# Second block: the normalised activations are split, and the conv taps read PSUM

## The chip, the cores and the metric

The kernel runs on one core of a Trainium2 chip. Each engine (TensorE or PE, VectorE or DVE, ScalarE or ACT, GpSimd or POOL, and SyncE or SP, which here mostly issues DMAs) works through its own queue in order and waits for the others at semaphores. The time is device microseconds (us) of one execution; the median of three runs stands for a kernel.

## What is computed

The reference runs two blocks and returns a normalised result. `first_block` has two layers of pooling, sparse attention and memory attention, all behind an RMS norm. The change lies in `second_block`:

```python
h_res = concat([meta_tokens (16), x (256)])             # T = 272 tokens, D = 1024
h = rmsnorm(h_res, norm1_w)                             # per token
q, k, v, z, b_raw, a_raw, sc_b, sc_c, sc_x, gate_a, gate_b = split(h @ w_in)
q, k, v = silu(depthwise_conv_centred([q, k, v], conv_w))    # 5 taps along tokens
q, k = l2norm(q), l2norm(k)
# gated delta rule, forward and backward, in chunks of 64:
#   decay, L = strict(beta * k k^T * decay), T = (I + L)^-1, state update per chunk
y_a = (norm(o_fwd + o_bwd) * silu(z)) @ w_branch_dn
y_b = (sc_b * depthwise_conv_centred(sc_c * sc_x, sc_conv_w)) @ w_branch_sc   # 3 taps
merged = sigmoid(gate_a) * y_a + sigmoid(gate_b) * y_b
h_res = h_res + merged @ w_out ;  then an MLP and a last norm
```

Everything is float32. Each product is made of three matmuls of a type that keeps fewer bits: both operands are split into a high part H and a low part L (value minus H), and H·H, H·L and L·H are summed in PSUM.

## The kernel before

Activations lie with channels on the 128 partitions (KT = 8 groups of 128) and tokens along the row. All weights come over SP's queue in pieces of 128x4x256 (`load`, L94, five buffers `raw`). `weights` splits each piece: `wH` is a copy on ScalarE (L107), `wL` the difference on VectorE, and for every third piece in block two on GpSimd (L110); four buffers each. `unit` and `unit2` make the product of one weight block with the split activations, 24 matmuls per half of 128 outputs (L123), into PSUM tiles `mm`, of which there are four. `units` (L151) does the same for two blocks together, k by k but the last two, so that work can begin before the last channels of x are there.

In `_block2` the operand is the split of x·fn and meta·n1, where `fn` is the product of two norm weights: **it is not divided by each token's root mean square yet**. The row `St` (L635) has that scale for all 272 tokens. It comes from squares summed over channels by a matmul with ones (`st`, L631), a root on ScalarE and a reciprocal on VectorE, while the first matmuls (`pk`, two blocks of k) run. Each result is then multiplied by St as it is taken from PSUM:

```python
V.tensor_tensor(r[:, a:], pss[i][:, :T - a], St[:, a:], op=OP.mult)      # rc, L672
ACT.activation(ac[:, lo:], r[:, lo:], AF.Copy, scale=w[:, 2:3])           # L680
ACT.activation(a4[:, lo:T - 2], r[:, lo + 2:], AF.Copy, scale=w[:, 4:5])  # L681
G.tensor_tensor(ac[:, lo:T - 2], ac[:, lo:T - 2], a4[:, lo:T - 2], op=OP.add)  # L682
```

and three more taps follow on VectorE (L685, result `ac` for q and k, `vf` for v). The twelve units of q, k and v have 24 halves, so 72 such taps. The same scaling is done for `ba` (L754), z (`zs`, L1167), the gates (L1161) and, in the short convolution, for `cS` on VectorE (L1188) and again on GpSimd (L1189, since sc_c and sc_x are multiplied) and for `cv` on GpSimd (L1201).

`delta()` is a generator that is advanced between units. It makes l2 norms (squares `l2s` L703, matmul `l2p` L705, logs and exponentials `rn`), the products `kq` (L713, every third on GpSimd), decays `E` (L897, L899) and the masked matrices (L909, L910, L923). The triangular inverse of the 32x32 corners follows: 31 pairs `tm` and `Tb` (L828, L830) on VectorE, and a small one for the meta tokens, `mt`, on GpSimd. The result, copied to `Lb` (L943), goes through memory and back over SP's queue (`sT` L946, `Tn` L998, `TBX` L1000, `TT` L1003), so that the larger inverse can begin on TensorE (`x`, L1016). Ahead of `x` stand the meta tokens' states: `mkv` (L976 on VectorE, L980 on ScalarE), `mvn` (L979) and `ms` (L984) on TensorE.

A scheduler sets the order of each engine's instructions when the program is built. It simulates the engines with a model of costs, so the order of the code and the order on an engine differ. The pool `ap2` of the second block takes the memory of the first block's pool, and its first writers are five DMAs that ScalarE issues (`cw` and others, L583); the pool of the split operand `xH`, `xL` exists from the start.

## Time and profile before

| | us |
|---|---|
| median of 3 runs | 1180.85 |
| the runs | 1182.15, 1174.7, 1180.85 |
| the profiled execution | 1179.4 |
| its span, first to last instruction | 1177.4 |
| TensorE busy | 1114.1 (95%) |
| VectorE busy | 869.0 (74%) |
| ScalarE busy | 586.7 (50%) |
| GpSimd busy | 383.5 (33%) |
| mean granted clock of TensorE | 0.979 |

Busy times add up instructions, and matmuls overlap, so a busy TensorE is not one at its peak. Block one ends near 571 us; block two's mixers run from there to about 940, with the MLP behind. The granted clock is a share of full speed (2.4 GHz; the lower level is 1.2).

### The profile page before, as it was taken

Reading aid. Unit: us, or ns where it says so; the run is one execution under the profiler, and the core shown is the slowest. Engines: PE = TensorE matmul, PEld = TensorE weight load, DVE = VectorE, ACT = ScalarE, POOL = GpSimd, SP = SyncE. Lnnn points to the kernel's source line nnn. Section 1 sums busy time; section 2 is a strip of 40 time slices with the busy share of each in tenths; the row PEclk is TensorE's granted clock in tenths of the full one; section 3 lists DMA queues with packets and bytes.
Section 4 is the critical chain, followed back from the end, with each engine's and each line's share of the span. In section 5 each row is a group of like instructions: output and inputs, shape, how many; then the busy total and the mean of one; then the engine's idle time right before and its main releaser. Section 6 shows DMA issues by size and latency. Waiting matters only on the chain.

```text
span 1177.4 us, 23260 instructions
## 1 busy us (share of the span) xinstructions
PE 1114.1 (95%) x9536; PEld 1086.1 (92%) x9536; DVE 869.0 (74%) x1220; ACT 586.7 (50%) x883; POOL 383.5 (33%) x304
## 2 busy tenths in 40 slices
...
GB/s 262 268 211 170 156 173 123 180 192 182 196 192 182 179 133 136 147 177 180 186 169 144 181 82 144 134 175 105 148 126 94 134 187 180 200 172 199 180 193 40
DMA packets 68514, 194.63 MB, mean 165 GB/s; under 512 B 19504, under 2 KB 21816, under 8 KB 67896
## 3 DMA queue, kind: packets, MB, share of 16 engines
...
q14 instruction: 32, 0.26, 0.1%
...
## 4 chain that ended last, share of the span: by engine, by line
PE 70%; DVE 17%; DMA 4%; issue 3%; ACT 2%; POOL 2%; SPq 1%; DVEq 0%; ACTq 0%; POOLq 0%
PE mm L123 49%; PE mml L151 8%; PE mmd L1302 5%; DVE wL L110 4%; DVE ac L685 2%; DVE Tb L830 1%; PE hp L372 1%; ACT wH L107 1%; DMA sT<-Lb 1%; DMA rows<-scr 1%; DVE tm L828 1%; DVE vf L685 1%; DVE kq L713 1%; PE mo L495 1%; PE vn L1088 1%
## 5 line engine op out<-in xcount | busy, mean ns | idle before, releaser
L110 DVE TENSOR_TENSOR wL<-raw,wH 128x1024 fp32r<-128x1024 f32 (+2 forms) x292 | 395.9, 1362 | 156.4 <-ACT wH L107 139.4
L107 ACT ACTIVATE wH<-raw 128x1024 fp32r<-128x1024 f32 (+3 forms) x347 | 347.0, 1034 | 302.4 <-PE mm L123 150.2
L123 PE MATMUL mm<-xH,wL 128*128 128x256 f32 (+3 forms) x1720 | 247.7, 284 | 11.2 <-DVE wL L110 11.2
L123 PE MATMUL mm<-xH,wH 128*128 128x256 f32 (+3 forms) x1720 | 249.0, 286 | 5.6 <-ACT ac L680 1.8
L123 PE MATMUL mm<-xL,wH 128*128 128x256 f32 (+3 forms) x1720 | 248.6, 285 | 0.0
L123 PEld LDWEIGHTS mm<-xH,wL 128*128 128x128 f32 (+1 forms) x1720 | 221.9, 190 | 13.5 <-DVE wL L110 12.3
L123 PEld LDWEIGHTS mm<-xH,wH 128*128 128x128 f32 (+1 forms) x1720 | 222.7, 190 | 9.5 <-ACT ac L680 2.0
L123 PEld LDWEIGHTS mm<-xL,wH 128*128 128x128 f32 (+1 forms) x1720 | 223.2, 191 | 2.8 <-issue 2.2
L110 POOL TENSOR_TENSOR wL<-raw,wH 128x1024 fp32r<-128x1024 f32 (+2 forms) x55 | 133.9, 2434 | 217.5 <-ACT wH L107 149.3
L397 POOL TENSOR_TENSOR bp<-bias,sc 128x1024 f32<-128x1024 f32 (+1 forms) x4 | 14.7, 3667 | 246.3 <-DVE sc L395 219.9
L123 PE MATMUL mm<-yH,wH 128*128 128x256 f32 x256 | 42.5, 286 | 4.9 <-ACT yH L1207 4.9
L123 PE MATMUL mm<-yL,wH 128*128 128x256 f32 x256 | 43.0, 286 | 4.3 <-DVE yL L1208 4.3
L123 PE MATMUL mm<-yH,wL 128*128 128x256 f32 x256 | 42.1, 285 | 0.0
L191 POOL TENSOR_TENSOR acc<-x 128x256 f32<-128x256 f32 x2 | 1.4, 722 | 123.6 <-DVE x L562 120.4
L123 PEld LDWEIGHTS mm<-yH,wH 128*128 128x128 f32 x256 | 35.6, 193 | 5.2 <-ACT yH L1207 5.1
L123 PEld LDWEIGHTS mm<-yL,wH 128*128 128x128 f32 x256 | 35.7, 193 | 5.1 <-DVE yL L1208 4.8
L123 PEld LDWEIGHTS mm<-yH,wL 128*128 128x128 f32 x256 | 35.5, 193 | 0.3 <-issue 0.3
L193 POOL TENSOR_TENSOR sq<-x 128x256 f32<-128x256 f32 x33 | 33.6, 1027 | 6.2 <-DVE x L562 5.5
L685 DVE SCALAR_TENSOR_TENSOR ac<-rc,cw,ac 128x271 f32<-128x271 f32 (+3 forms) x48 | 34.4, 753 | 0.0
L191 POOL TENSOR_TENSOR a<-x 128x256 f32<-128x256 f32 x3 | 2.8, 941 | 80.4 <-DVE x L562 74.8
L1302 PE MATMUL mmd<-aH,wH 128*128 128x256 f32 x176 | 28.6, 281 | 0.0
L1302 PE MATMUL mmd<-aH,wL 128*128 128x256 f32 x176 | 28.6, 281 | 0.0
...
## 6 DMA issues: line engine op xcount, KB each, us to landing
...
```

Source lines behind the costliest of these rows:

```text
L107: nc.scalar.activation(H, raw, AF.Copy)
L110: e.tensor_tensor(L, raw, H.bitcast(F32), op=OP.subtract)
L123: self.last_mm = nc.tensor.matmul(ps, lt(a, kt), rt(b, kt), start=i == 0, stop=i == n - 1).ins
L151: self.last_mm = self.nc.tensor.matmul(ps[:, :N], w[a](k)[:, h * 128:h * 128 + 128], xs[b][:, k, :], start=k == 0 and (a, b) == (0, 0), st ...
L193: nc.gpsimd.tensor_tensor(tmp, x, x, op=OP.mult)
L372: nc.tensor.matmul(pp[p][:, j, :n], a[r, 2 * i + j, :], b(r, 2 * i + j), start=True, stop=True)
L397: nc.gpsimd.tensor_tensor(bp[:, :, :n], bias[:, :, off:], pen[:, None, :n].to_broadcast([128, 8, n]), op=OP.add)
L495: nc.tensor.matmul(ps[:, h, :], mv[:, mb, h * 128:h * 128 + 128], PT[:, mb, h, :], start=mb == 0, stop=mb == 1)
L685: V.scalar_tensor_tensor(ac[:, t0:t1], r[:, t0 + j - 2:t1 + j - 2], w[:, j:j + 1], ac[:, t0:t1], op0=OP.mult, op1=OP.add)
L713: (V if (i * 8 + h) % 3 else G).tensor_tensor(t, t, sl(h, i), op=OP.mult)
L828: eng.tensor_tensor(t, Lb[:, j + 1:, j:j + 1].to_broadcast([P, m, w]), Tb[:, j:j + 1, 0:w].to_broadcast([P, m, w]), op=OP.mult)
L1302: nc.tensor.matmul(pss[h][:, :S], w[a](k)[:, h * 128:h * 128 + 128], (aH, aL)[b][:, k0 + k, :], start=k0 + k == 0 and (a, b) == (0, 0), st ...
```

## The change

The operand of the first two k blocks stays as it was, under the name `uHL` and in a place of the pool `ap2` that is used by `kq` later; their results alone are still scaled by St. As soon as St is there, `scaled_operand` makes the split of x·fn·St, which every other unit uses. Their results need no scaling, so the taps read PSUM, z and `cS` become copies on ScalarE, the gates' tanh reads PSUM, and the scalings on GpSimd go. GpSimd's add of `a4` moves behind the three taps.

```diff
@@ -597,11 +597,13 @@
 
     fn = sp.tile([128, KT], F32, tag="fn", name="fn")
     V.tensor_tensor(fn, fg, n1, op=OP.mult)
-    xH, xL = K.operand(0, T, T)
+
+    uHL = ap.tile([128, 2 * KT * T], F32R, tag="kq", name="uHL")
+    uH, uL = (uHL[:, i:i + KT * T].rearrange("p (k t) -> p k t", k=KT) for i in (0, KT * T))
     for k in range(KT):
-        K.scaled_hl(xH[:, k, 0:16], xL[:, k, 0:16], meta[:, k, :], n1[:, k:k + 1])
+        K.scaled_hl(uH[:, k, 0:16], uL[:, k, 0:16], meta[:, k, :], n1[:, k:k + 1])
     for k in range(KT):
-        K.scaled_hl(xH[:, k, 16:], xL[:, k, 16:], x[:, k, :], fn[:, k:k + 1])
+        K.scaled_hl(uH[:, k, 16:], uL[:, k, 16:], x[:, k, :], fn[:, k:k + 1])
     St = ap.tile([128, T], F32, tag="St", name="St")
     S1 = sp.tile([128, S], F32, tag="Sx", name="S1")
     a1 = sp.tile([128, S], F32, tag="acc", name="a1")
@@ -634,6 +636,17 @@
         K.tab(sd[:, 16:], ps[:, 16:T], AF.Sqrt, bias=e2, scale=1.0 / D)
         V.reciprocal(St, sd)
 
+    def scaled_operand():
+
+        xH, xL = K.operand(0, T, T)
+        for k in range(KT):
+            t = ap.tile([128, T], F32, tag="t1", name="xt", bufs=2)
+            V.scalar_tensor_tensor(t[:, 0:16], meta[:, k, :], n1[:, k:k + 1], St[:, 0:16], op0=OP.mult, op1=OP.mult)
+            V.scalar_tensor_tensor(t[:, 16:], x[:, k, :], fn[:, k:k + 1], St[:, 16:], op0=OP.mult, op1=OP.mult)
+            ACT.activation(xH[:, k, :], t, AF.Copy)
+            V.tensor_tensor(xL[:, k, :], t, xH[:, k, :].bitcast(F32), op=OP.subtract)
+        return xH, xL
+
 
     xd = K.dp.tile([128, KT, S], F32, tag="xd", name="xd")
     nc.scalar.dma_start(out=xd, in_=x)
@@ -658,18 +671,21 @@
 
     def qkv(which, u, pss=None, flush=True):
 
+        raw = pss is not None
         if pss is None:
             pss = unit2(A["w_qkv"][which * 4 + u], 256, 14 if which == 0 else 0)
 
         alt = u % 2 if which < 2 else 0
-        rc = ap.tile([128, 2, T], F32, tag=("b4", "LT64")[alt], name="rc", bufs=3 - 2 * alt)
+        if raw:
+            rc = ap.tile([128, 2, T], F32, tag=("b4", "LT64")[alt], name="rc", bufs=3 - 2 * alt)
         acs = ap.tile([128, 2, T], F32, tag="t2", name="ac", bufs=2) if which < 2 else None
         lo = 16 if which == 0 else 0
         for i in range(2):
             h = 2 * u + i
             a = 14 if which == 0 else 0
-            r = rc[:, i, :]
-            V.tensor_tensor(r[:, a:], pss[i][:, :T - a], St[:, a:], op=OP.mult)
+            if raw:
+                V.tensor_tensor(rc[:, i, :], pss[i][:, :T], St, op=OP.mult)
+            r = lambda t0, t1: rc[:, i, t0:t1] if raw else pss[i][:, t0 - a:t1 - a]
             if which < 2:
                 ac = acs[:, i, :]
                 a4 = ap.tile([128, T], F32, tag="t1", name="a4", bufs=2)
@@ -677,13 +693,13 @@
                 ac = vf[:, h, :]
                 a4 = ap.tile([128, T], F32, tag="sgt", name="a4", bufs=2)
             w = cw[:, which * 8 + h, :]
-            ACT.activation(ac[:, lo:], r[:, lo:], AF.Copy, scale=w[:, 2:3])
-            ACT.activation(a4[:, lo:T - 2], r[:, lo + 2:], AF.Copy, scale=w[:, 4:5])
-            G.tensor_tensor(ac[:, lo:T - 2], ac[:, lo:T - 2], a4[:, lo:T - 2], op=OP.add)
+            ACT.activation(ac[:, lo:], r(lo, T), AF.Copy, scale=w[:, 2:3])
+            ACT.activation(a4[:, lo:T - 2], r(lo + 2, T), AF.Copy, scale=w[:, 4:5])
             for j in (0, 1, 3):
                 t0, t1 = max(lo, 2 - j), min(T, T + 2 - j)
-                V.scalar_tensor_tensor(ac[:, t0:t1], r[:, t0 + j - 2:t1 + j - 2], w[:, j:j + 1], ac[:, t0:t1],
+                V.scalar_tensor_tensor(ac[:, t0:t1], r(t0 + j - 2, t1 + j - 2), w[:, j:j + 1], ac[:, t0:t1],
                                        op0=OP.mult, op1=OP.add)
+            G.tensor_tensor(ac[:, lo:T - 2], ac[:, lo:T - 2], a4[:, lo:T - 2], op=OP.add)
             if which < 2:
                 silus.append((kq[:, h, 1 - which, lo:], ac[:, lo:]))
         if flush:
@@ -742,8 +758,9 @@
         V.scalar_tensor_tensor(y, p, 2.0, y, op0=OP.mult, op1=OP.add)
         V.scalar_tensor_tensor(g, y, -1.0, bc3(ea), op0=OP.mult, op1=OP.mult)
 
-    pk = K.units([A["w_qkv"][4], A["w_qkv"][5]], (xH, xL), KT, 2, N=T)
+    pk = K.units([A["w_qkv"][4], A["w_qkv"][5]], (uH, uL), KT, 2, N=T)
     scales()
+    xH, xL = scaled_operand()
     K.rstd(S1, a1, S, 1.0 / D)
 
     qkv(1, 0, pk[0:2], flush=False)
@@ -751,7 +768,7 @@
 
     pba = unit2(A["w_ba"], 48, 0)[0]
     ba = ap.tile([48, T], F32, tag="b4", name="ba", bufs=3)
-    V.tensor_tensor(ba, pba[:48, :T], St[:48, :], op=OP.mult)
+    V.tensor_copy(ba, pba[:48, :T])
     tok = ap.tile([128, 3, 48], F32, tag="tok", name="tok")
     G.memset(tok, 0.0)
     ps = K.pat.tile([128, 3, 48], F32, tag="at", name="tokp")
@@ -1149,7 +1166,6 @@
     K.add_side(dl)
 
     xx = (xH[:, :, 16:], xL[:, :, 16:])
-    Sx = St[:, 16:]
     mg = K.mp.tile([128, KT, S], F32, tag="mg", name="mg2")
 
     def gate(which, g):
@@ -1158,13 +1174,12 @@
             out = ap.tile([128, 2, S], F32, tag="sgt", name="sgt", bufs=2)
         else:
             out = ga[g // 2][:, 2 * (g % 2):2 * (g % 2) + 2, :]
-        V.tensor_tensor(out, ps, _bc(Sx, 2), op=OP.mult)
-        K.tab(out, out, AF.Tanh, scale=0.5)
+        K.tab(out, ps, AF.Tanh, scale=0.5)
         return out
 
     def z_unit(g_):
         ps = K.unit(A["w_z"][g_], xx, KT, 256)
-        V.tensor_tensor(zs[:, 2 * g_:2 * g_ + 2, :], ps, _bc(Sx, 2), op=OP.mult)
+        ACT.activation(zs[:, 2 * g_:2 * g_ + 2, :], ps, AF.Copy)
         done.append("z")
         K.pump(K.rate)
 
@@ -1185,8 +1200,7 @@
             cS = [None, None]
             for i in range(2):
                 cS[i] = ap.tile([128, 258], F32, tag="c1", name="cS", bufs=2)
-                V.tensor_tensor(cS[i], pc[i][:, :258], St[:, 14:], op=OP.mult)
-                G.tensor_tensor(cS[i], cS[i], St[:, 14:], op=OP.mult)
+                ACT.activation(cS[i], pc[i][:, :258], AF.Copy)
             K.pump(K.rate)
             px = unit2(A["w_sc"][2, u], 256, 14)
             cv = [None, None]
@@ -1198,7 +1212,6 @@
                 for j, n in ((0, S), (2, S - 1)):
                     V.scalar_tensor_tensor(cv[i][:, :n], cS[i][:, 1 + j:1 + j + n], scw[:, k, j:j + 1], cv[i][:, :n],
                                            op0=OP.mult, op1=OP.add)
-                G.tensor_tensor(cv[i], cv[i], Sx, op=OP.mult)
             K.pump(K.rate)
             pb = K.unit(A["w_sc"][0, u], xx, KT, 256)
             for i in range(2):
```

Lines behind 600 are numbered differently after it: taps L700, GpSimd's add L702, `xt` L644 and L645, xH L646, xL L647, `mkv` L997.

The scheduler's order at three places. First, ScalarE at the start of block two. Before (block one's `sq` and `a` are sums of squares, `xd` a copy of x to memory):

```order
L185 ACTIVATE xH<-x,fn 128x256 x3
L107 ACTIVATE wH<-raw 128x1024 x2
L583 DMA cw<-in_dn_conv 128x120
L583 DMA scw<-in_sc_conv 128x24
L583 DMA dnw<-in_dn_norm 128x1
L583 DMA tri<-in_const 128x256
L583 DMA adt<-in_adt 128x32
L185 ACTIVATE xH<-x,fn 128x256
L618 ACTIVATE a_6848<-x,vec_82 128x256
L621 ACTIVATE sq_6865<-x,vec_82 128x256
L621 ACTIVATE sq_6871<-x,vec_82 128x256
L639 DMA xd<-x 128x2048
```

After, with `uHL` both parts of the first operand:

```order
L107 ACTIVATE wH<-raw 128x1024 x8
L583 DMA cw<-in_dn_conv 128x120
L583 DMA scw<-in_sc_conv 128x24
L583 DMA dnw<-in_dn_norm 128x1
L583 DMA tri<-in_const 128x256
L583 DMA adt<-in_adt 128x32
L185 ACTIVATE uHL<-meta,vec_82 128x16 x8
L185 ACTIVATE uHL<-x,fn 128x256 x8
L620 ACTIVATE a_6847<-x,vec_82 128x256
L623 ACTIVATE sq_6864<-x,vec_82 128x256
L623 ACTIVATE sq_6870<-x,vec_82 128x256
```

The copies for the operand stood ahead of the DMAs and among block one's last work, all but the last; now all 16 stand behind the DMAs, and the squares behind them.

Second, VectorE from St on. Before:

```order
L635 RECIPROCAL St<-sd 128x272
L672 TENSOR_TENSOR rc<-mml,St 128x272 x4
L110 TENSOR_TENSOR wL<-raw,wH 128x1024
L754 TENSOR_TENSOR ba<-mm_7096,St 48x272
L110 TENSOR_TENSOR wL<-raw,wH 128x1024
L204 RECIPROCAL S_6846<-sd 128x256
L685 SCALAR_TENSOR_TENSOR ac<-rc,cw,ac 128x270
L672 TENSOR_TENSOR rc<-mm_7175,St 128x272
L685 SCALAR_TENSOR_TENSOR ac<-rc,cw,ac 128x270 x2
L762 COPY tok<-tokp 128x96
L763 COPY tok<-tokp 16x48
L685 SCALAR_TENSOR_TENSOR ac<-rc,cw,ac 128x270
```

After (`xt` is the normalised x of one k, in two parts):

```order
L637 RECIPROCAL St<-sd 128x272
L644 SCALAR_TENSOR_TENSOR xt<-meta,vec_82,St 128x16
L645 SCALAR_TENSOR_TENSOR xt<-x,fn,St 128x256
L644 SCALAR_TENSOR_TENSOR xt<-meta,vec_82,St 128x16
L645 SCALAR_TENSOR_TENSOR xt<-x,fn,St 128x256
L687 TENSOR_TENSOR rc<-mml,St 128x272 x4
L204 RECIPROCAL S_6845<-sd 128x256
L647 TENSOR_TENSOR xL<-xt,xH 128x272 x2
...
L645 SCALAR_TENSOR_TENSOR xt<-x,fn,St 128x256
L644 SCALAR_TENSOR_TENSOR xt<-meta,vec_82,St 128x16
L645 SCALAR_TENSOR_TENSOR xt<-x,fn,St 128x256
L647 TENSOR_TENSOR xL<-xt,xH 128x272 x2
```

The split of the normalised x stands between the scaling of the first two blocks and their taps, where ba's scaling and the next weights' low parts were; the last xt follows all twelve taps.

Third, ScalarE from the copy of Lb on, where `mkv` is the second of the two meta states. Before:

```order
L107 ACTIVATE wH<-raw 128x1024 x2
L1197 ACTIVATE cv<-cS,scw 128x256
L980 ACTIVATE mkv<-mvn 16x512
L107 ACTIVATE wH<-raw 128x1024 x2
L1197 ACTIVATE cv<-cS,scw 128x256
L985 ACTIVATE Sf_9349<-ms 128x512
L107 ACTIVATE wH<-raw 128x1024 x2
L980 ACTIVATE mkv<-mvn 16x512
L1207 ACTIVATE yH<-cv 128x256 x2
L985 ACTIVATE Sf_9375<-ms 128x512
```

After:

```order
L107 ACTIVATE wH<-raw 128x1024 x2
L1203 ACTIVATE cS<-mm_9655 128x258
L997 ACTIVATE mkv<-mvn 16x512
L1211 ACTIVATE cv<-cS,scw 128x256
L1002 ACTIVATE Sf_9348<-ms 128x512
L107 ACTIVATE wH<-raw 128x1024 x2
L1211 ACTIVATE cv<-cS,scw 128x256
L997 ACTIVATE mkv<-mvn 16x512
L107 ACTIVATE wH<-raw 128x1024 x2
L1002 ACTIVATE Sf_9374<-ms 128x512
```

Between the first mkv and the second stood two groups of two wH; now it is one.

## Rows read from the trace of the kernel before

**Rows 1.** The page: busy time of each engine (us, share of the span, instructions), and the chain that ended last, by engine.

```profile
PE 1114.1 (95%) x9536; PEld 1086.1 (92%) x9536; DVE 869.0 (74%) x1220; ACT 586.7 (50%) x883; POOL 383.5 (33%) x304
...
PE 70%; DVE 17%; DMA 4%; issue 3%; ACT 2%; POOL 2%; SPq 1%; DVEq 0%; ACTq 0%; POOLq 0%
```

**Rows 2.** Windows of the span: from:to and length in us; busy us and instructions of PE, PEld, DVE, ACT and POOL in turn; TensorE's granted clock as a share of full speed; mean busy share of the DMA engines; GB/s.

```profile
606.00:645.00 39.00, 34.26 (x260) 32.94 (x259) 38.87 (x77) 24.77 (x48) 19.55 (x16) 0.96 0.44 149
645.00:680.00 35.00, 30.35 (x218) 28.25 (x217) 29.73 (x44) 33.38 (x62) 22.40 (x16) 0.96 0.50 168
680.00:720.00 40.00, 34.43 (x228) 32.88 (x228) 40.00 (x47) 23.43 (x40) 25.53 (x24) 0.86 0.32 92
720.00:760.00 40.00, 27.25 (x217) 26.07 (x215) 37.56 (x44) 17.59 (x31) 37.74 (x37) 0.95 0.51 149
805.00:832.00 27.00, 20.00 (x150) 18.06 (x154) 11.67 (x20) 7.41 (x12) 4.52 (x4) 0.79 0.59 158
832.00:938.00 106.00, 105.57 (x1246) 102.53 (x1239) 61.31 (x98) 48.29 (x62) 15.74 (x6) 0.97 0.32 104
```

**Rows 3.** VectorE's groups by line between the first kq product and the copy of Lb, 673.6:805.3 (busy us, mean ns of one; idle before).

```profile
L110 DVE TENSOR_TENSOR wL<-raw,wH 128x1024 fp32r<-128x1024 f32 x20 | 32.7, 1634 | 0.1
L830 DVE TENSOR_TENSOR Tb<-Tb,tm 128x31 f32<-128x31 f32 (+15 forms) x31 | 22.0, 711 | 0.7
L685 DVE SCALAR_TENSOR_TENSOR vf<-rc,cw,vf 128x271 f32<-128x271 f32 (+1 forms) x12 | 18.1, 1529 | 0.0
...
L713 DVE TENSOR_TENSOR kq<-kq,rn 128x272 f32<-128x272 f32 (+1 forms) x10 | 8.7, 934 | 0.0
```

**Rows 4.** Single lines: the durations of one instruction, min/median/max in ns, and the starts of the first and the last (VectorE in 673.6:805.3; the last is TensorE's weight load for l2p).

```profile
L685 DVE SCALAR_TENSOR_TENSOR vf<-rc,cw,vf x12: 478/487/7427, 683.4 to 711.6; 128x271 f32<-128x271 f32 x8, 128x270 f32<-128x270 f32 x4
...
L110 DVE TENSOR_TENSOR wL<-raw,wH x20: 1206/1223/4047, 683.9 to 798.3; 128x1024 fp32r<-128x1024 f32 x20
...
L713 DVE TENSOR_TENSOR kq<-kq,rn x10: 410/959/2589, 673.6 to 682.2; 128x272 f32<-128x272 f32 x5, 128x256 f32<-128x256 f32 x5
...
L830 DVE TENSOR_TENSOR Tb<-Tb,tm x31: 193/390/5054, 743.8 to 804.0; 128x31 f32<-128x31 f32 x2, 128x60 f32<-128x60 f32 x2, 128x87 f32<-128x87 f32 x2, 128x112 f32<-128x112 f32 x2
...
L672 DVE TENSOR_TENSOR rc<-mm,St x3: 420/427/428, 678.1 to 691.2; 128x272 f32<-128x272 f32 x3
...
L705 PEld LDWEIGHTS l2p<-l2s,ones x32: 186/189/190, 643.9 to 667.2; 128*128 128x128 f32 x32
```

**Rows 5.** Timeline of VectorE, then of GpSimd, around 695 us (start us, duration us; xN is a run of N equal instructions).

```profile
694.61 7.43 DVE L685 SCALAR_TENSOR_TENSOR vf<-rc,cw,vf 128x270 f32<-128x270 f32 x1
...
703.17 0.90 DVE L685 SCALAR_TENSOR_TENSOR vf<-rc,cw,vf 128x270 f32<-128x270 f32 x2
...
694.76 1.89 POOL L897 TENSOR_TENSOR E<-Gb,Gt 128x1024 f32<-128x1024 f32 x1
...
699.41 2.33 POOL L110 TENSOR_TENSOR wL<-raw,wH 128x1024 fp32r<-128x1024 f32 x1
```

**Rows 6.** Timeline at the start of the second block: TensorE, ScalarE (an earlier place, then the start; ACTq is a DMA issue on its queue), VectorE.

```profile
571.19 0.92 PE L151 MATMUL mml<-xH,wH 128*128 128x272 f32 x6
...
546.50 1.68 ACT L185 ACTIVATE xH<-meta,vec 128x16 fp32r<-128x16 f32 x8
...
571.39 0.38 ACTq L583 DMA_DIRECT2D cw<-in_dn_conv  x1
...
573.89 0.51 ACT L185 ACTIVATE xH<-x,fn 128x256 fp32r<-128x256 f32 x1 [1.70 <-DVE x L562]
...
585.20 1.85 DVE L635 RECIPROCAL St<-sd 128x272 f32<-128x272 f32 x1 [0.36 <-ACT sd L89]
```

**Rows 7.** Timeline of TensorE: a unit's first group, and the groups around an idle time.

```profile
594.23 1.17 PE L123 MATMUL mm<-xH,wH 128*128 128x272 f32 x8
...
608.00 1.33 PE L123 MATMUL mm<-xH,wH 128*128 128x258 f32 x8 [1.83 <-ACT ac L680]
...
612.47 1.11 PE L123 MATMUL mm<-xH,wH 128*128 128x258 f32 x8
613.42 1.12 PE L123 MATMUL mm<-xL,wH 128*128 128x258 f32 x8
```

**Rows 8.** GpSimd's groups by line in 673.6:805.3.

```profile
L1189 POOL TENSOR_TENSOR cS<-cS,St 128x258 f32<-128x258 f32 x7 | 5.7, 818 | 20.2 <-DVE cS L1188 16.0 <-PE mm L123 4.3
L1201 POOL TENSOR_TENSOR cv<-cv,St 128x256 f32<-128x256 f32 x6 | 5.6, 936 | 5.6 <-DVE cv L1199 5.6
```

**Rows 9.** Timeline from the copy of Lb to x: VectorE, SP's queue, ScalarE, TensorE.

```profile
804.27 1.03 DVE L943 COPY Lb<-Tb 128x1024 f32<-128x1024 f32 x1
...
819.79 3.33 SPq L1003 DMA_DIRECT2D TT<-sT  x4
...
828.08 1.06 ACT L107 ACTIVATE wH<-raw 128x1024 fp32r<-128x1024 f32 x1 [8.01 <-DMA raw<-in_w_gate]
829.04 0.57 ACT L980 ACTIVATE mkv<-mvn 16x512 f32<-16x512 f32 x1
...
829.67 2.07 PE L984 MATMUL ms<-mkv 16*128 16x128 f32 x8 [5.46 <-ACT mkv L980]
831.67 0.26 PE L1016 MATMUL x<-Tn,LT 32*32 32x32 f32 x1
```

## The prediction

> **What bounds the kernel now.** I read the page first [rows 1]: TensorE is busy 95% of the span, and the chain that ended last lies 70% on it, but 17% on VectorE. The windows [rows 2] say where those 17% are. In 832:938 TensorE is busy 105.57 of 106 us. Before that it lacks 4.7 us in 606:645, 4.7 in 645:680, 5.6 in 680:720, 12.8 in 720:760 and 7.0 in 805:832, and its granted clock is 0.79 to 0.96 of full speed. In the same stretches VectorE is busy 38.87 of 39, 40.00 of 40 and 37.56 of 40 us; GpSimd's share rises to 37.74 in 720:760. So the second block's convolutions and triangular inverse run at VectorE's pace, and what lies around them at TensorE's.
>
> Why VectorE is slow there is in its lines between the first kq product and the copy of Lb [rows 3] against the spread of single durations [rows 4]. A tap (L685) has a median of 487 ns and a mean of 1529; the low part wL (L110) 1223 and 1634; the kq products 410 at best and 934 on average; the inverse's L830 390 and 711. I call the excess over the short durations stretch. The timeline shows one: the tap at 694.61 takes 7.43 us, while GpSimd is busy without a gap from 694.76 until its wL ends at 701.7 [rows 5]. In contrast rc, which reads PSUM, never stretched: 420 to 428 ns [rows 4]. Of the 72 taps, 60 become instructions that read PSUM.
>
> **The change, part by part.** All sums are made against the profiled execution: span 1177.4, device time 1179.4, so 2 us lie outside the span. The median of the three runs is 1180.85; they spread over 0.6%, and about 1% is what a measurement can tell from no change.
>
> *Start of the block: a loss.* Before, x is split under block one's last matmuls, and TensorE goes into xH at 571.19 without a gap [rows 6]. After, uHL lies in the pool that opens with the second block, and its 16 copies on ScalarE stand behind five DMA issues (first order fence). Those begin at 571.39, because the first waits for TensorE, and ScalarE's next instruction starts at 573.89 [rows 6]. Then come eight narrow copies (1.68 us together) and the first wide one (0.51): the first matmul starts near 576.0, a gap of 4.8 us. After a gap the clock falls: from 608.00, after 1.83 us idle, three groups of eight matmuls take 4.47 us, where the next group takes 0.95 from start to start [rows 7], 1.6 us lost. Together 6.4: St starts near 591.6, not 585.20, and is there at 593.4.
>
> *The second split: a loss.* After St, VectorE's rows hold 8 narrow and 8 wide xt, 4 rc, the reciprocal for S, 12 taps and six xL ahead of the last xt's successor on ScalarE (second fence). Taps of SBUF last 0.48 at best, two in a row 0.90, so each overlaps the next by some 0.07 [rows 4, 5]. With narrow xt at 0.2 (as on ScalarE), wide xt and taps at 0.48, rc and xL at 0.42 and S at St's 1.85, it is 17.3 us less 39 overlaps, 14.6; the last xH 0.5 later, near 608.5. GpSimd's instructions in this stretch could lengthen it by a few us; I take none, since its four adds come behind the taps. TensorE has by then run 22 of the 72 matmuls of ba and the next unit, as each xH comes; 50 remain: 50 x 0.95/8 = 5.9 us, and 1.6 for the clock. That unit ends near 616, where the next one's began at 594.23 before [rows 7]: **22 us late.**
>
> *Most of this is regained by the first kq product.* Before, the way from 594.2 to the last l2p at 667.2 took 73 us, at VectorE's pace, and 6.4 more to the first kq product at 673.6 [rows 4]. By the orders, TensorE has 128.8 thousand columns between st and the last l2p, against 143.5. From 616, past the first 20 thousand, the remaining 109 at 258 columns in 0.119 us need 50 us: 666. VectorE's work shrinks below that: the mean of a tap falls from rows like 1529 to about 450, and the rc are gone. ScalarE is full (33.38 of 35 in 645:680, [rows 2]) and its silus now wait for GpSimd's add behind the taps; I allow 8 us of waits, between none and the 13 that TensorE has before in 606:680 with its clock. So the first kq product is at 666+8+6.4 = 680, **6.5 late.**
>
> *From there to the copy of Lb: the gain.* Before 673.6 to 805.3, 131.6 us [rows 4, 9]. The stretch in it, from [rows 3, 4]: taps 18.1−12×0.485 = 12.3; wL 32.7−20×1.22 = 8.3; kq 8.7−10×0.41 = 4.6; L830 22.0−31×0.39 = 9.9. Removed outright: 3 rc, 7 cS and 2 zs of double width at rc's price, 5.9, less overlaps 5.0. The taps' 12.3 goes; but GpSimd still has its burst, and the next VectorE instruction with two SBUF operands will meet it, so I let half of it come back there. GpSimd loses L1189 and L1201, 5.7+5.6 us [rows 8] of 88, 13%, so the other 22.8 shrink by 3. Sum: −12.3+6.2−3.0−5.0 = −14.1. The copy of Lb ends at 680+117.5 = 797.5, **7.8 early.** The ends of this term: −5 (all stretch returns elsewhere) and −29 (the taps' goes, and half of the rest).
>
> *From there to x at 831.67.* Before, the transfers of Lb and Tb fill SP's queue until the four TT from 819.79, and only then come weights of the gate. ScalarE waits 8.01 us for one, its mkv copy stands behind that at 829.04, and TensorE sits idle 5.46 until ms at 829.67 [rows 9]. After, this mkv copy stands two weights earlier on ScalarE (third fence) and queues behind no load from after the transfers: −5.5; the clock's fall behind the gap goes with it, −1.6 to −2. But x stands 7.9 thousand columns earlier among TensorE's instructions, so 3.6 us of matmuls that ran ahead of it now follow. Together −3.8. Behind x both kernels are TensorE-bound [rows 2], with the same matmuls.
>
> *With one answer each.* ScalarE's copies out of PSUM for zs and cS: twelve of some 0.5 to 0.6 us (its mkv copy out of PSUM takes 0.57, [rows 9]), hidden on an engine that is busy 23.43 of 40 us in 680:720; uncovered 6 us. The gates' scaling was VectorE's, behind x, where TensorE is the bound: nothing. GpSimd's add behind the taps: in its queue wL and E stand behind it, which then wait for VectorE's three taps, 1.3 us; within the waits above.
>
> Sum: −7.8−3.8 = −11.6 on 1179.4, rounded **1167**.
>
> **A page that speaks against it.** Taps that read PSUM are priced by rc's 0.42 beside 0.48 for the best SBUF tap [rows 4]; reading PSUM costs nothing there. The Trainium skill, page "VectorE: DVE Perf Modes", section "Rules for kernel authors", advises to accept the slowest mode for elementwise work on a matmul's output, or to copy to SBUF first if many operations follow; here five follow and the copy is taken away. By rc's rows no faster mode is lost, and by that rule the sum would be worse only by what a faster mode would have saved in the taps, of which the trace shows nothing.
>
> **Rivals.** (a) *More stretch goes*: GpSimd's work finds few partners left; the −29 end, 1179.4−22.6−3.8 = 1153. For it: a third of the stretch sits at taps, and the burst's longest meeting is one. Against: wL and the inverse keep theirs.
>
> (b) *The stretch only moves*: the burst falls on the wL or E behind the tap, −5.0 in place of −14.1, with the same late start: 1177. For it: GpSimd keeps 87% of its work, and VectorE stays full. The Trainium skill, page "SBUF — State Buffer", section "SBUF: two separate sides", says that a VectorE operation with two SBUF inputs and a GpSimd operation that reads SBUF lock one pair of ports against each other, and the loser waits for the whole instruction. The 7.43 us beside rc's 0.42 agree; by it the taps are free of the lock, and whichever instruction with two SBUF inputs comes next is not.
>
> (c) *The 22 us are regained less*: the orders let TensorE wait for ScalarE as it did for VectorE; first kq at 690: 1178.
>
> (d) *Slower: PSUM is held too long.* A result was free after one rc of 0.42 us. Now two ScalarE copies and three taps hold it, and the copy to a4 stands behind silus that wait for GpSimd's add of the unit before. Of four buffers a unit takes two, so TensorE stops once this ring takes longer than two units, 2×48×0.119 = 11.4 us. The ring's own work (two copies of 0.5, three taps of 0.42, GpSimd's add of about 1, a silu of 0.4, for two halves) is some 7 us, so it holds unless ScalarE's or VectorE's other work gets between. If it breaks, the price is that of 608.00, 1.83 idle and 1.6 of clock, at each of ten units: 34 us, against a gain of 12: 1191 to 1202.
>
> (e) *It does not free the taps*: taps stretch with a PSUM operand too. Then nothing is gained between kq and Lb but the 5, and the result is that of (b).
>
> **How the numbers follow.** Forecast, 1156 to 1169: 0.34. (a) below 1156: 0.13. (b), (c) and (e), 1169 to 1190: 0.36. (d): 0.17. So faster by over 1% (below 1169.0) 0.47, within it 0.36, slower by over 1% (above 1192.7) 0.17. The range 1149 to 1188 leaves out most of (d) and a little of (a); the likeliest case's own is 1156 to 1169.
>
> **What the profile after would show.** A gap of some 5 us on TensorE before uHL; St near 593; TensorE fed piece by piece until 608; no tap of several us among those that read PSUM; first kq near 680, Lb's copy near 797; no ScalarE wait for the gate's weights ahead of mkv; equal lengths from x on. If wL, E or yL grow by what the taps lose, it is (b). If TensorE waits for ac or a4 at each unit, it is (d). What would make me most wrong is an order that waits where I counted engines as free, since every wait here is between queues that run in order.

## The result and the profile after

The changed kernel takes 1195.3 us, the median of four runs (1193.7 to 1197.7), where the kernel before took 1181.5 beside it: ratio 1.0128, 95% interval 1.0081 to 1.0175. It is 1.3% slower. I had forecast 1167 and a range up to 1188.

The page after, as in [rows 1]: busy time of each engine, and the chain by engine.

```profile
span 1191.1 us, 23261 instructions
...
PE 1118.3 (94%) x9536; PEld 1088.9 (91%) x9536; DVE 846.1 (71%) x1204; ACT 592.5 (50%) x903; POOL 367.3 (31%) x288
...
PE 74%; DVE 12%; issue 4%; ACT 4%; DMA 3%; POOL 2%; SPq 1%; DVEq 0%; POOLq 0%; ACTq 0%
```

VectorE did lose work: 869.0 to 846.1 us, and its share of the chain fell from 17% to 12%. TensorE gained none of that. Its idle time (span less busy) rose from 63.3 to 72.8, and its busy time by 4.2 with the same 9,536 matmuls. Those 9.5 and 4.2 are the 13.7 us by which the span grew.

To see where, I cut both traces at the same instructions (starts, in us; the last E product is the last `E<-kkq,E`, L910 before and L927 after, where `kkq` are TensorE's products of k with k and q; the last step runs to the end of the span):

| | first kq | from kq to the last E product | to the copy of Lb | to the end | span |
|---|---|---|---|---|---|
| before | 673.6 | 49.1 | 81.6 | 373.1 | 1177.4 |
| after | 684.8 | 62.4 | 67.9 | 376.0 | 1191.1 |
| difference | +11.2 | +13.3 | −13.7 | +2.9 | +13.7 |

The forecast had +6.5, then −14.1 for the two middle steps together, then −3.8. By these marks a gain of 13.7 stands behind the last E product and a loss of 13.3 ahead of it. Part of that is one thing counted at both marks: when the last E product comes late, work that stood behind it has run ahead of it (TensorE runs some 60 matmuls fewer behind it). From the first step of the inverse (tm, 742.42 before and 762.98 after) to the copy of Lb it is 61.9 and 52.1 us, so 9.8 of the 13.7 lie in the inverse itself.

The marks are VectorE's. What TensorE lost by them is its idle time (length less busy) in the same stretches:

| TensorE idle, us | to the first kq | from kq to the copy of Lb | to the end | sum |
|---|---|---|---|---|
| before | 19.3 | 24.6 | 19.4 | 63.3 |
| after | 33.8 | 19.8 | 19.1 | 72.8 |

So all that TensorE waits more lies ahead of the first kq product. Between kq and Lb it waits 4.8 us less, a third of the 14 that I had booked there.

**The first step.** Windows of the kernel after, the two stretches from the start of block two (columns as in [rows 2]):

```profile
569.00:616.00 47.00, 29.84 (x196) 27.66 (x197) 35.74 (x76) 25.16 (x53) 19.53 (x24) 0.82 0.38 128
616.00:684.00 68.00, 63.20 (x475) 61.09 (x474) 50.13 (x101) 53.94 (x108) 33.63 (x25) 0.97 0.49 172
```

and the first of them in the kernel before:

```profile
569.00:616.00 47.00, 44.77 (x345) 43.91 (x345) 42.96 (x74) 32.38 (x56) 31.40 (x34) 0.96 0.56 191
```

In the first stretch TensorE is busy 29.84 of 47 us at a granted clock of 0.82, where it was 44.77 at 0.96. In the second it is busy 63.20 of 68 (before 60.44): little of what was lost can be regained there. The idle times, from the timeline of TensorE after; then ScalarE at the first of them, and VectorE at the third:

```profile
573.54 5.81 PE L151 MATMUL mml<-uHL,wH 128*128 128x272 f32 x32 [4.59 <-POOL sqm L613]
...
591.82 1.21 PE L123 MATMUL mm<-xH,wH 128*48 128x272 f32 x6 [3.55 <-ACT xH L646]
598.24 1.59 PE L123 MATMUL mm<-xH,wH 128*48 128x272 f32 x6 [5.21 <-ACT xH L646]
603.32 1.59 PE L123 MATMUL mm<-xH,wH 128*48 128x272 f32 x6 [3.49 <-ACT xH L646]
```

```profile
571.35 1.70 ACT L185 ACTIVATE uHL<-meta,vec 128x16 fp32r<-128x16 f32 x8 [1.72 <-issue]
...
572.95 3.29 ACT L185 ACTIVATE uHL<-x,fn 128x256 fp32r<-128x256 f32 x8
```

```profile
597.78 0.48 DVE L645 SCALAR_TENSOR_TENSOR xt<-x,fn,St 128x256 f32<-128x256 f32 x1
598.18 1.73 DVE L700 SCALAR_TENSOR_TENSOR ac<-rc,cw,ac 128x271 f32<-128x271 f32 x4
...
602.32 0.48 DVE L645 SCALAR_TENSOR_TENSOR xt<-x,fn,St 128x256 f32<-128x256 f32 x1
```

At 573.54 the profile names `sqm`, but the first wide copy to uHL, which TensorE needs too, ended only just before (572.95 and an eighth of 3.29). The three waits for xH are 12.3 us. Between two pairs of xt stand taps and the xL that must free the two places of the ring.

**The middle steps.** VectorE's groups between the first kq and the copy of Lb after, as in [rows 3]:

```profile
L110 DVE TENSOR_TENSOR wL<-raw,wH 128x1024 fp32r<-128x1024 f32 x21 | 27.9, 1334 | 3.6 <-ACT wH L107 3.5
L1213 DVE SCALAR_TENSOR_TENSOR cv<-cS,scw,cv 128x256 f32<-128x256 f32 (+1 forms) x12 | 18.2, 1519 | 0.0
L847 DVE TENSOR_TENSOR Tb<-Tb,tm 128x31 f32<-128x31 f32 (+15 forms) x31 | 14.8, 479 | 0.7
...
L916 DVE SCALAR_TENSOR_TENSOR E<-E 128x1024 f32<-128x1024 f32 x3 | 10.1, 3357 | 1.6 <-POOL E L914 1.6
...
L700 DVE SCALAR_TENSOR_TENSOR vf<-mm,cw,vf 128x271 f32<-128x271 f32 (+1 forms) x12 | 5.6, 491 | 0.1
```

The taps on PSUM are 491 ns on average where they were 1529, as foreseen; wL fell from 1634 to 1334 and the inverse's line from 711 to 479. But the short convolution's taps `cv`, which read SBUF, now average 1519 and E 3357. The same two in the kernel before, 673.6:805.3:

```profile
L1199 DVE SCALAR_TENSOR_TENSOR cv<-cS,scw,cv 128x256 f32<-128x256 f32 (+1 forms) x12 | 5.5, 483 | 0.0
L899 DVE SCALAR_TENSOR_TENSOR E<-E 128x1024 f32<-128x1024 f32 x3 | 3.9, 1288 | 0.0
```

Now the stretch in which the last E products wait, VectorE after:

```profile
709.20 6.95 DVE L916 SCALAR_TENSOR_TENSOR E<-E 128x1024 f32<-128x1024 f32 x1 [1.58 <-POOL E L914]
...
725.34 1.27 DVE L927 TENSOR_TENSOR E<-kkq,E 128x512 f32<-128x512 f32 x2
729.89 0.43 DVE L1209 TENSOR_TENSOR cS<-mm,cS 128x258 f32<-128x258 f32 x1 [3.28 <-ACT cS L1203]
733.77 1.23 DVE L110 TENSOR_TENSOR wL<-raw,wH 128x1024 fp32r<-128x1024 f32 x1 [3.45 <-ACT wH L107]
...
735.79 0.68 DVE L926 TENSOR_TENSOR At<-kkq,E 128x512 f32<-128x512 f32 x1
736.39 4.81 DVE L1213 SCALAR_TENSOR_TENSOR cv<-cS,scw,cv 128x255 f32<-128x255 f32 x1
...
742.32 0.68 DVE L927 TENSOR_TENSOR E<-kkq,E 128x512 f32<-128x512 f32 x1
...
747.18 0.68 DVE L927 TENSOR_TENSOR E<-kkq,E 128x512 f32<-128x512 f32 x1
```

And what those waits are for, ScalarE after, then the last group of kkq on TensorE, after, before and in the run e24 below:

```profile
725.47 1.28 ACT L89 ACT_TABLE_LOAD   x1
726.76 2.30 ACT L89 ACTIVATE vf<-vf 128x544 f32<-128x544 f32 x4
...
729.49 0.37 ACT L1203 ACTIVATE cS<-mm 128x258 f32<-128x258 f32 x1
...
747.89 0.42 ACT L934 ACTIVATE LT<-E 64x256 f32<-64x256 f32 x1 [5.25 <-DVE E L927]
```

```profile
730.41 1.89 PE L923 MATMUL kkq<-kq 128*128 128x256 f32 x8
```

```profile
714.59 1.89 PE L906 MATMUL kkq<-kq 128*128 128x256 f32 x8
```

```profile
720.58 1.89 PE L926 MATMUL kkq<-kq 128*128 128x256 f32 x8
```

After the change the last kkq has been in PSUM since 732.3. VectorE takes its E product at 742.32 and 747.18, because the short convolution stands ahead of it: `cS`, a copy which ScalarE now makes behind a table load and five silus, a wL whose wH stands behind that, and a `cv` of 4.81 us. ScalarE then waits 5.25 us for the product. This is not the whole of the 13.3: from the first kq product to the start of that kkq group it is 45.6 us after and 41.0 before, and from there to the last E product 16.8 and 8.1. So 8.7 of it arise in VectorE's queue and 4.6 on TensorE, which ran 360 matmuls between kq and the last E product where it ran 276. While that `cv` ran, GpSimd was busy nearly all the time:

```profile
735.97 2.36 POOL L110 TENSOR_TENSOR wL<-raw,wH 128x1024 fp32r<-128x1024 f32 x1
738.29 0.28 POOL L847 TENSOR_TENSOR mt<-mt 8x48 f32<-8x48 f32 x1
738.54 2.38 POOL L947 TENSOR_TENSOR kq<-kq,Gb 128x1024 f32<-128x1024 f32 x1
740.88 0.43 POOL L845 TENSOR_TENSOR mt<-mt 8x39 f32<-8x39 f32 x1
```

### The profile page after: what moved, and what is told of

Same layout as the page of the kernel before. It is cut to its first block, busy times and chain, and to the rows that moved or that the text cites. A ratio compares the mean times of both kernels' runs of the same rounds, so it can differ in the third digit from the quotient of the medians.

```text
span 1191.1 us, 23261 instructions
## 1 busy us (share of the span) xinstructions
PE 1118.3 (94%) x9536; PEld 1088.9 (91%) x9536; DVE 846.1 (71%) x1204; ACT 592.5 (50%) x903; POOL 367.3 (31%) x288
## 3 DMA queue, kind: packets, MB, share of 16 engines
q8 instruction: 74, 1.21, 0.4%
## 4 chain that ended last, share of the span: by engine, by line
PE 74%; DVE 12%; issue 4%; ACT 4%; DMA 3%; POOL 2%; SPq 1%; DVEq 0%; POOLq 0%; ACTq 0%
PE mm L123 53%; PE mml L151 7%; PE mmd L1315 5%; DVE wL L110 3%; ACT wH L107 1%; PE hp L372 1%; DMA sT<-Lb 1%; DVE ac L700 1%; DVE cv L1213 1%; DVE kq L729 1%; DMA raw<-in_w_a 1%; PE mo L495 1%; PE o L1136 1%; PE vn L1105 1%; PE mqk L473 1%
## 5 line engine op out<-in xcount | busy, mean ns | idle before, releaser
L123 PE MATMUL mm<-xH,wH 128*128 128x256 f32 (+3 forms) x1720 | 252.5, 288 | 20.2 <-ACT xH L646 12.6
L123 PE MATMUL mm<-xH,wL 128*128 128x256 f32 (+3 forms) x1720 | 248.7, 286 | 10.9 <-DVE wL L110 9.3
L123 PEld LDWEIGHTS mm<-xH,wH 128*128 128x128 f32 (+1 forms) x1720 | 225.2, 193 | 26.4 <-ACT xH L646 13.9
L123 PEld LDWEIGHTS mm<-xH,wL 128*128 128x128 f32 (+1 forms) x1720 | 222.8, 191 | 14.1 <-DVE wL L110 11.3
L110 POOL TENSOR_TENSOR wL<-raw,wH 128x1024 fp32r<-128x1024 f32 (+2 forms) x55 | 131.2, 2386 | 250.7 <-ACT wH L107 173.6
L397 POOL TENSOR_TENSOR bp<-bias,sc 128x1024 f32<-128x1024 f32 (+1 forms) x4 | 14.7, 3677 | 246.2 <-DVE sc L395 220.4
L1315 PE MATMUL mmd<-aL,wH 128*128 128x256 f32 x176 | 28.6, 281 | 0.0
```

The source lines that it names most:

```text
L110: e.tensor_tensor(L, raw, H.bitcast(F32), op=OP.subtract)
L123: self.last_mm = nc.tensor.matmul(ps, lt(a, kt), rt(b, kt), start=i == 0, stop=i == n - 1).ins
L397: nc.gpsimd.tensor_tensor(bp[:, :, :n], bias[:, :, off:], pen[:, None, :n].to_broadcast([128, 8, n]), op=OP.add)
L1315: nc.tensor.matmul(pss[h][:, :S], w[a](k)[:, h * 128:h * 128 + 128], (aH, aL)[b][:, k0 + k, :], start=k0 + k == 0 and (a, b) == (0, 0), st ...
```

## Experiments

All are edits of the changed kernel unless another is named, and times are beside runs of the kernel before (1181 to 1182). Letters of theories are those of the expectations.

**The start.** First `uHL` goes back to the place of xH and xL, which exists from the start of the kernel; then each xt gets a place of its own as well; then that alone.

```diff
-    uHL = ap.tile([128, 2 * KT * T], F32R, tag="kq", name="uHL")
-    uH, uL = (uHL[:, i:i + KT * T]...)
+    uH, uL = K.operand(0, T, T)                                     # e1, e2
...
-            t = ap.tile([128, T], F32, tag="t1", name="xt", bufs=2)
+            t = vf[:, k, :]                                         # e2, e3
```

> The changed kernel, but the un-normalised operand of the first two units goes into the buffer of xH and xL, as before the change, so that it is split under block one's last matmuls; the normalised one overwrites it once those units are through. Theory A (what TensorE loses at the start of block two is lost for good, since TensorE bounds what follows): the gap of 4.6 us before the first matmul of block two and about 1 us of low clock go, so 1195.3 - 5.6 = about 1190. Theory B (the loss is made behind the first kq product and behind x, by ScalarE's new copies and the stretch that moved to other instructions; what is won at the start is waited away there): within 3 us of 1195.

> As the one with the early operand, and xt is written to eight places (the not yet used vf) in place of two, so that VectorE makes all sixteen xt in a row behind St, ahead of rc, S and the taps. By the order the last xt ends some 4.5 us after St, not 15. Theory A: TensorE's waits for xH fall from 12.6 to about 5 us and their low clock with them (3 us), so 1190 - 10 = about 1180, no slower than the kernel before. Theory B: 1190 to 1195.

> The changed kernel with the eight places for xt alone; the first operand stays in the late pool. Theory A: 1195.3 - 10 = about 1185. Theory B: 1192 to 1197.

Measured: 1189.3 (ratio 1.0075, 1.0048 to 1.0101), 1183.8 (1.0029, 1.0017 to 1.0040) and 1191.9 (1.0079, 1.0058 to 1.0099). e1 came out as theory A had it. With both, the first kq is at 680.0, the last E product 58.3 behind it, and 11.5 us of the loss are gone. But e2 missed its 1180, and e3, with 3.5 us in place of theory A's 10, lies at the edge of theory B's range. TensorE's waits from 569 to 1010 in e2 (in total, times, longest) show why:

```profile
PE mm L123 <- DVE ac L699: 10.9, 1, 10.9
PE ms L1000 <- ACT mkv L996: 5.3, 1, 5.3
...
PE mm L123 <- ACT xH L645: 3.3, 1, 3.3
```

The waits for xH shrank from 12.6 to 3.3, and a single wait of 10.9 for a tap, which holds PSUM, stands in their place (3.8 in the changed kernel): rival (d), once, and not at each unit. In e3 that wait is 10.8.

**Do taps on PSUM pay, and are ScalarE's copies the cause?** In e4 VectorE copies every q, k and v result to SBUF and the taps read that; in e5 it makes the copies of z and cS.

```diff
+                V.tensor_copy(rc[:, i, a:], pss[i][:, :T - a])      # e4: every unit not scaled by St
...
-        ACT.activation(zs[:, 2 * g_:2 * g_ + 2, :], ps, AF.Copy)
+        V.tensor_copy(zs[:, 2 * g_:2 * g_ + 2, :], ps)              # e5
...
-                ACT.activation(cS[i], pc[i][:, :258], AF.Copy)
+                V.tensor_copy(cS[i], pc[i][:, :258])                # e5
```

> The changed kernel, but the results of all units of q, k and v are first copied by VectorE from PSUM to SBUF, without a scale, and the taps read SBUF as before the change: 20 more copies of 0.42 us on VectorE, and 60 taps that can stretch again. If the taps' freedom from stretch is worth something on the path: 12 us of stretch between kq and Lb come back and the time is 1200 to 1207. If stretch only goes from one instruction to the next and TensorE is the bound: 1193 to 1199.

> The changed kernel, but the copies of z and of cS out of PSUM are made by VectorE, as their scaling was before the change; all else stays. In the trace of the changed kernel VectorE waits 3.3 us for cS, which ScalarE makes behind Exp, a table load and seven Silu, and ScalarE waits 21 us for cS products in turn. Theory C (the gain behind the first kq product was lost to ScalarE's new copies standing in its queue): 5 to 8 us faster, 1188 to 1190, and the way from the first kq product to the copy of Lb, 130.3 us, falls to about 124. Theory D (it was lost to stretch that moved from the taps to E and cv while GpSimd's burst stayed): within 3 us of 1195, and that way stays within 3 us.

Measured: 1199.8 (1.0154, 1.0135 to 1.0173) and 1193.5 (1.0096, 1.0073 to 1.0120). e4 lies at the edge between its two ranges: in this order of the work, taps on PSUM are worth some 4.5 us, and not 12. That sum holds the 20 copies and the stretch together (the taps average 1334 ns again, `cv` still 1394). The engine that copies z and cS is worth some 2, so theory C falls (e12 against e9, below: 1.4).

**GpSimd's add.** The prediction had priced its move behind the taps at nothing. In e6 it goes back ahead of them; in e23 for q and k alone, in e24 for v alone. In e17 it stays behind, and a4 has four buffers.

```diff
+            G.tensor_tensor(ac[:, lo:T - 2], ac[:, lo:T - 2], a4[:, lo:T - 2], op=OP.add)
             for j in (0, 1, 3):
...
-            G.tensor_tensor(ac[:, lo:T - 2], ac[:, lo:T - 2], a4[:, lo:T - 2], op=OP.add)
```

> The changed kernel, but GpSimd's add of a4 stands ahead of the three taps, as before the change. Theory: GpSimd's adds behind the taps hold up silus and GpSimd's own queue: then 3 to 6 us faster, 1189 to 1192. Rival: with the add first the taps wait for GpSimd again, which is busy without a gap for up to 9 us near 705 to 716, and PSUM is held for as long: 3 to 8 us slower, 1198 to 1203.

> The changed kernel with four buffers in place of two for a4 of q and k; GpSimd's add stays behind the taps. With the add moved back ahead of the taps the kernel was 9.6 us faster. Theory E (that came from the ring: ScalarE's copy to a4 waits for GpSimd's add of the unit before, which waits for VectorE's taps, so ScalarE's whole queue waits): most of it comes here too, 1186 to 1190. Rival F (it came from the order in which GpSimd's work meets VectorE's, or from what the scheduler put elsewhere): 1193 to 1197.

> The changed kernel with GpSimd's add of a4 ahead of the three taps for q and k alone; v's adds stay behind. With the add first everywhere the time was 1185.7, 9.6 below the changed kernel. Theory S (the gain is at the start: behind the waiting taps of the first two k units VectorE could no longer hold up the last xt and xL, so that TensorE's wait for xH shrank from 12.6 to 7.3 and the last xt came earlier): nearly all of it stays here, 1185 to 1188, first kq near 685, the way from kq to the copy of Lb about 118 to 122. Theory V (the gain is at v's taps, where GpSimd's adds decide whether its burst meets E or wL): 1192 to 1196, way from kq to Lb near 131, E still long.

> The other half: the add ahead of the taps for v alone. Theory S: 1193 to 1196, TensorE's wait for xH stays near 12.6 and E near 3.4 us on average. Theory V: 1185 to 1188, with the wait for xH as in the changed kernel, E near 1.5 on average and the way from kq to the copy of Lb near 118. If each half gives some 5 (1190 both), both places count.

Measured: e6 1185.7 (1.0031, 1.0015 to 1.0046), e17 1196.4 (1.0122, 1.0103 to 1.0140), e23 1194.3 (1.0104, 1.0088 to 1.0121), e24 1186.8 (1.0046, 1.0031 to 1.0061). So the add is worth 9.6, more than the 3 to 6 that I expected, the ring of q and k is not how, and v's eight adds carry 8.5 of it: theory V. e17 left v's two buffers of a4 as they were; no run gave v more, but in 684:750 of the changed kernel's trace no wait of ScalarE is put down to GpSimd's add. Theory S falls although e23 did what it said: the waits for xH fell to 7.3, but a wait of 6.8 for a tap came in their place.

VectorE in e24, the same place as above:

```profile
717.94 4.83 DVE L110 TENSOR_TENSOR wL<-raw,wH 128x1024 fp32r<-128x1024 f32 x1
...
731.83 1.27 DVE L929 TENSOR_TENSOR At<-kkq,E 128x512 f32<-128x512 f32 x2
733.02 0.48 DVE L702 SCALAR_TENSOR_TENSOR vf<-mm,cw,vf 128x271 f32<-128x271 f32 x1
733.43 1.27 DVE L930 TENSOR_TENSOR E<-kkq,E 128x512 f32<-128x512 f32 x2
739.26 0.43 DVE L1212 TENSOR_TENSOR cS<-mm,cS 128x258 f32<-128x258 f32 x1 [4.56 <-ACT wH L107]
```

The last E products stand ahead of cS, and the wait of VectorE falls behind them. From the first kq to the last E product it is 44.4 us instead of 62.4. Most of these 18 us come from TensorE's order and not from VectorE's: the last kkq group starts 31.0 us behind kq, where it was 45.6, with 210 matmuls in the stretch in place of 360; from that group to the last E product it is 13.4 instead of 16.8. The stretch has not gone: wL averages 1951 ns where it was 1334, E 1548 where it was 3357. The whole way from kq to the copy of Lb is 116.3 (start to start), 14.4 below before: the size I had forecast. But kq itself is at 689.6, 4.8 later than in the changed kernel, so Lb comes 9.2 earlier, and the time is still 0.5% above the kernel before.

**Both repairs, and a third unit ahead of the split.** e11 is e2 with the add first. In e9, ba and the third unit of k use the un-normalised operand too, so that TensorE has work while x is split; e13 is e9 with the add first, e12 is e9 with z and cS copied by VectorE, e14 is e13 with four buffers of a4.

```diff
+    pba = unit2(A["w_ba"], 48, 0, (uH, uL))[0]
+    p12 = unit2(A["w_qkv"][6], 256, 0, (uH, uL))
...
-    V.tensor_copy(ba, pba[:48, :T])
+    V.tensor_tensor(ba, pba[:48, :T], St[:48, :], op=OP.mult)
...
-    qkv(1, 2)
+    qkv(1, 2, p12)
```

> Early operand, eight places for xt, and GpSimd's add ahead of the taps. Alone the first two gave 1183.8 and the third 1185.7, from 1195.3. If the losses add up (11.5 and 9.6): 1174 to 1177, faster than the kernel before. If both sit at the same place (TensorE's wait for PSUM at 600 to 620 is 10.9 us in the first and 6.8 in the second): 1181 to 1184.

> The kernel with the early operand and eight places for xt, in which also ba and the third unit of k use the un-normalised operand and are scaled by St as they leave PSUM (three evictions with a multiplication more), so that TensorE has 9 us of work while St and the normalised split are made. Theory A (the start is what was lost): TensorE's waits for xH fall to under 2 us and its clock stays up; 1183.8 - 4 - 2 = about 1178, faster than the kernel before by 0.2 to 0.4%. Theory B: 1183 to 1185, as without it.

> The kernel with ba and three units of k on the un-normalised operand, and the copies of z and cS made by VectorE. Theory C: 4 to 7 us faster than with ScalarE's copies. Theory D: within 3 us of it.

> As before, and ba and three units of k on the un-normalised operand. In its version with the add behind the taps TensorE waits once 13.2 us for the taps of a unit, since ScalarE's a4 copy waits 5.1 us for GpSimd's add. Theory E: that wait falls below 6 us and the time to 1174 to 1178. Rival F: 1183 to 1186.

> As the one with three units of k and the add first, and four buffers for a4. With the add first the ring is short, so within 2 us of it if theory E holds; if ScalarE still waits for GpSimd's add there, 3 to 5 us faster.

Measured: e11 1181.2 (0.9989, 0.9970 to 1.0009), e9 1185.5 (1.0031, 1.0015 to 1.0046), e12 1184.1 (1.0019, 1.0003 to 1.0035), e13 1181.2 (0.9999, 0.9982 to 1.0016), e14 1182.8 (1.0019, 1.0003 to 1.0035). With the start and the add mended the loss is gone, 14 us, though the two repairs alone sum to 21. The add brings 9.6 in the changed kernel, but 2.6 on top of e2 (e11) and 4.3 on top of e9 (e13). The traces show where the rest stays: from e2 to e11 x comes 13.0 us earlier (832.1 to 819.1), and the stretch behind x becomes 12.0 longer (348.7 to 360.7). e13 shows it against the kernel before. Its first kq is at 680.2 and its copy of Lb starts at 798.1, close to where I had them, and x is at 816.9, even earlier than my forecast. The windows from x to the end, before and in e13 (columns as in [rows 2]):

```profile
831.70:1177.40 345.70, 334.00 (x3178) 328.55 (x3177) 200.81 (x242) 155.54 (x193) 132.05 (x73) 0.98 0.47 151
```

```profile
816.90:1177.30 360.40, 346.05 (x3294) 341.80 (x3293) 205.97 (x247) 162.08 (x203) 136.37 (x75) 0.99 0.49 158
```

x stands 14.8 us earlier and the stretch behind it is 14.7 longer, with 116 matmuls more in it: nothing is left.

e9 missed its 1178 with a wait of 13.2 us for a tap; e13 missed theory E's 1174 to 1178 with one of 11.1, which was to fall below 6, and F's range too. The wait in e13, on TensorE, and the engine that holds the tile:

```profile
623.82 2.06 PE L123 MATMUL mm<-xH,wH 128*128 128x258 f32 x8 [11.05 <-DVE ac L701]
```

```profile
611.19 3.37 DVE L701 SCALAR_TENSOR_TENSOR ac<-rc,cw,ac 128x271 f32<-128x271 f32 x3
...
623.18 1.68 DVE L701 SCALAR_TENSOR_TENSOR ac<-mm,cw,ac 128x271 f32<-128x271 f32 x4
```

The unit's taps come one by one between weights and decays, and its PSUM is free only after the last, near 623.8.

**Free PSUM at once.** On e13, VectorE copies results out of PSUM with one instruction each, for two units (e19) or for all of q and k behind the third (e20). e22 does two units on the changed kernel; e25 is e20 with the add behind.

```diff
+        cp = not raw and which < 2                       # e20; e19, e22: two named units
-        if raw:
+        if raw or cp:
             rc = ap.tile([128, 2, T], F32, ...)
...
+            if cp:
+                V.tensor_copy(rc[:, i, a:], pss[i][:, :T - a])
```

> The version with three blocks of k on the un-normalised operand, eight places for xt and the add first, in which VectorE copies the results of two units (the fourth of k, the first of q) out of PSUM and their taps read SBUF. In that version TensorE waits once for 11.1 us, at 612.8, for PSUM that these two units hold until ScalarE has loaded a table, made silus and begun their taps. Theory G (reading PSUM directly makes TensorE wait for ScalarE's queue; with the evictions of before PSUM was free after 0.42 us): that wait falls below 4 us, its low clock of 1.7 us goes, and the time is 1181.2 - 8 = 1171 to 1175. Rival H (TensorE is early there and waits for the same work at the next place): the wait moves and the time stays within 2 us, 1179 to 1183.

> As the one with two units copied, but all units of q and k that the taps would read from PSUM are copied first; v, z and cS still leave PSUM directly. Theory G: no wait for ac anywhere; 1171 to 1177, with the risk that 8 us more of VectorE and taps that stretch again cost 2 to 4 us against the two copies. Rival H: 1180 to 1186.

> The changed kernel itself with the first two units behind ba (third and fourth of k) copied out of PSUM by VectorE. There TensorE comes late and waits only 3.8 us for ac. Theory G: 1 to 4 us faster, 1191 to 1194. Rival H: 1194 to 1197.

> The fastest version so far (1176.05: operand of the first units from the start of the kernel, eight places for xt, three units un-normalised, all other q and k results copied out of PSUM by VectorE, add first) with the add behind the taps. It tells whether the add's place is worth anything once PSUM is freed at once. Theory S or V with a price of its own: 1182 to 1186. Theory P (the add's place mattered through the time for which PSUM and the ring behind it were held): 1175 to 1178.

Measured: e19 1186.8 (1.0049, 1.0029 to 1.0069), e20 **1176.1** (0.9957, 0.9941 to 0.9973), e22 1194.8 (1.0114, 1.0085 to 1.0143), e25 1177.0 (0.9955, 0.9938 to 0.9971). For two units the wait only moves, as in theory H, but e19 is 5.5 us slower than e13, outside both ranges; e22 lies within the noise of the changed kernel (theory H). For all of q and k it goes (theory G). TensorE's longest waits in e20, 569 to 1010:

```profile
PE mm L123 <- DVE wL L110: 7.6, 3, 3.8
PE mm L123 <- DVE rc L690: 5.4, 2, 4.6
PE t L1045 <- DVE TBX L1039: 3.4, 1, 3.4
```

None is above 4.6 us. e20 and e25 are 0.4% faster than the kernel before, both intervals below 1. They keep the idea for v, z, the gates and the short convolution; q and k leave PSUM in one instruction each, as before the change. There the add's place no longer counts in the time (e25 against e20: 1.0, inside the spread of either), as theory P said. Its reason is not shown: v, which carried the add's price, reads PSUM in both. And the add still moves the order: Lb is copied at 803.3 in e25 and at 793.8 in e20, x comes at 822.2 and 812.8, and the stretch behind x takes 350.0 and 360.2. 9.4 us at x are worth nothing here.

## Why the prediction was wrong

*Start, +6.4 by St.* The gap was 4.59 for 4.8 forecast, from the cause that I named. St came 3.6 late and not 6.4, but block one ended some 2 us earlier in this trace, for which I have no reason.

*The second split, unit end 22 late.* The last xt started near 604.8 and the last xH ended near 605.8, where I had 608.5; the next unit began at 612.91 instead of 594.23, 18.7 late. That step was right, and a little too pessimistic, since St came earlier than I had it.

*"Most of this is regained by the first kq product".* This failed: +11.2, not +6.5. I let TensorE make up 15.5 of 22 us as the bound of this stretch. It made up 7.5 of 18.7. The term that was mis-sized is TensorE's own work. Window from that unit's start to the last l2p, and TensorE's group for l2p in it (columns as in [rows 2] and [rows 3]), both after:

```profile
612.90:678.00 65.10, 60.30 (x449) 57.96 (x448) 47.85 (x96) 49.97 (x104) 32.56 (x24) 0.97 0.52 184
```

```profile
L721 PE MATMUL l2p<-l2s,ones 128*128 128x272 f32 (+1 forms) x32 | 8.9, 389 | 0.9 <-ACT l2s L719 0.9
```

It worked 60.30 us and was idle 4.8, where I had 50 and 8. Priced by its columns like the rest, l2p came to some 4 us in my sum (32 of 272 or 256 columns, at 0.119 us for 258). Its operands are plain float32, and it takes more: the 8.9 of its busy time overlap with its neighbours, but the four in a row from 666.75 and one matmul behind them take 1.04 us from start to start, so some 0.23 each and 7.4 in all. That is a third of the 10; the rest is spread over the small products and the matmuls of the units. From the last l2p to kq took 7.2 for 6.4.

*"From there to the copy of Lb: the gain", −14.1.* The step failed at −0.4. Two of its terms were right: the taps' stretch went, and the inverse became 9.8 us shorter. What failed is that I summed stretch over a window as if any of it could go or stay with the same effect. VectorE's work there fell to 119.03 of 131.3 us (before 128.03 of 131.7), so it now waits. The orders that came with the change put the last kkq group later on TensorE (4.6 us), and `cS`, `wL` and `cv` ahead of the last E products on VectorE (8.7), which the inverse waits for. In e24, and in e6, e11, e13 and e14, which have the add first for q and k too, the way from kq to Lb is 116.3 to 117.9, so the gain can be had. I had shown the order at three places, none of them this.

*"GpSimd's add behind the taps: ... within the waits above".* This failed: 9.6 us (e6), 8.5 of it at v (e24). In 684:750 no wait of GpSimd itself is put down to a tap. But the add's place moves the whole order that follows. Which part of that order carries the price stays open: e24 changed TensorE's order as well as VectorE's, and no run moved the last E products alone.

*From Lb to x, −3.8.* The wait of mkv for the gate's weights did go, and x was only 2.1 late after a copy of Lb 10.8 late: −8.7, better than forecast. *"From x on equal"* failed: behind x the kernel lost 11.6. From x to the end TensorE was busy 340.43 us with 3,209 matmuls, where it had 334.00 with 3,178 (windows 833.8:1191.1 and 831.7:1177.4), and idle 16.9 where it had 11.7; in 832:938 it was busy 102.70 of 106 us (before 105.57). I had priced the work that ran ahead of x at 3.6 us. This step would have spoilt the forecast even with those above mended: in e13 kq, Lb and x come as early as forecast or nearly so, and the 116 matmuls more that then stand behind x take all of it back. A mark on VectorE's chain is not the time. The span is TensorE's busy and idle time together, and its idle time was 63.3 us before, 72.8 in the changed kernel, 64.2 in e13 and 61.0 in e20.

*Rivals.* (a) did not come. (b) held in part: E and cv took the taps' stretch, and its 1177 had the late start smaller than it was. (c) held in part: the first kq came at 684.8, between my 680 and its 690. The Trainium skill, page "SBUF — State Buffer", section "SBUF: two separate sides", has a VectorE operation with two SBUF inputs and GpSimd lock a port pair for a whole instruction. The 4.81 us of cv beside GpSimd's wL and kq agree with a lock, but outlast one instruction of GpSimd. The measured time lies within (d)'s 1191 to 1202, but by luck: there is no wait at ten units in the changed kernel, where TensorE waits 3.8 us for taps in all, but one of 11 us as soon as the late start no longer hid it (e2, e13). (e) falls: taps on PSUM took 491 ns.

*The sum.* 1179.4 less 11.6 is 1167.8, which rounds to 1168 and not to 1167, and the 1191 at (d)'s lower end is not worked out.
